# A second set of modulation vectors on TensorE, and the dense layer's first weights loaded one stage earlier

## The chip, the cores and the metric

The kernel runs on one core of a Trainium2 chip. The metric is the device time of one execution in microseconds (us). Five engines work side by side, each through its own instructions in order: TensorE (PE in the profile, with PEld for the loading of its weights), VectorE (DVE), ScalarE (ACT), GpSimd (POOL) and SyncE (SP), which issues most of the DMA transfers.

## The reference

Two layers of a diffusion backbone work on 512 latent and 256 context tokens of 1024 channels, in float32. Each layer is modulated by six vectors that come from a conditioning vector, one set for the latent tokens and one for the context:

```python
mod = silu(c) @ w_ada[l] + b_ada[l]            # 1024 x 6144, and the same with c_ctx
sh1, sc1, g1, sh2, sc2, g2 = split(mod, 6)
h = rms_norm(x, norm1_g[l]) * (1 + sc1) + sh1
p = split_cols(h @ w_in[l], GROUP_COLS)
y = [hgrn2(p[0]), rwkv7(p[1]), window_attention(p[2]), latent_attention(p[3])]
x = x + g1 * (concat(y) @ w_out[l])
h2 = rms_norm(x, norm2_g[l]) * (1 + sc2) + sh2
x = x + g2 * (swiglu(h2) if l == 0 else moe_swiglu(h2))
```

hgrn2 and rwkv7 are recurrences over the tokens, in both directions. The dense SwiGLU of layer 0 has 2816 hidden units; layer 1 has eight experts, of which each token takes two. The output is the final RMSNorm of the latent tokens.

## The kernel before, in words

The activations lie channels x tokens: eight tiles of 128 channels and 768 tokens. Large products are made of three passes: each operand is split into a high part (a cast on ACT, L259) and a low part (the difference, a subtraction on VectorE or POOL, L260), and `mm3` (L270) adds high x high, low x high and high x low. The passes stand as L272, L273 and L274 in the profile. `load_split` (L262) loads a weight tile of 512 KB (`raww`, by SP's queue) and splits it into `hiw` and `low`.

Layer 0 goes through these stages, in times of the profile: modulation, norm and input projection (to about 288); the recurrences of both directions, the attentions' preparation beside them (about 289 to 579); the attentions and the first two columns of the output projection (580 to 745); the other six columns with gated residuals (745 to 806); the second norm and the dense SwiGLU (806 to 1372). Layer 1 and its experts follow.

The modulation vectors are 48 channel tiles for each layer. They are computed in two ways.

- `ada` (L395) uses TensorE. Its weights are `wada`, groups of four channel tiles. The two conditioning vectors are the weights of a matmul of 32 columns, and four such matmuls use the four column quarters of the array, each for every fourth part of the sum (L406, tiles 128x32). ACT copies the four partial sums (L410, `adams`), TensorE transposes them (L413), and VectorE adds the quarters up (L417) and adds the bias (L418). Groups 0 to 3, the first norm's vectors, come at the start of the layer; groups 4 and 5 (the gate g1) come in `modulation` (L1398), beside the recurrences.
- `ada_rest` (L420) uses VectorE. Its weights are `wadt`, one channel tile of 128x1024 each, and the sum is one scaled sum (L436) for each of the two vectors with the vector spread over all partitions (`cb`). `spread` (L314) makes the two `cb` at the first step: 16 transposes (L319) into four PSUM tiles. It has 72 tiles: 24 for the second half of layer 0 (`mod2`: sh2, sc2, g2), 48 for layer 1. 16 of them come in the output projection, by the numbers of `AD` (L1277), the other 56 in the dense layer.

`weave` (L241) lays the streams of the recurrences stage into one program: RWKV's two directions one step a round each, HGRN and the attentions' preparation a fraction of a step, the modulation 6 steps in 122 rounds. The framework's scheduler then orders the instructions of each engine by the buffers and dependencies, and each engine goes through its list in order. A buffer of a pool comes free when its last reader is done; a pool opened on memory that others held waits for those.

In `mixers` (L1502 to L1521) the output projection loads the weights of a column and the input of its residual (`xo`), multiplies, adds the residual on VectorE (L1271), and collects the squares for the norm (`sumsq`). `ffn` (L1526) opens its own weight pool `fw`, loads the first three weight tiles, makes the norm's factors (`norm_rs`, L467 to L472) and its modulated tiles (`norm`, L490 to L492: `hhi` on ACT, `hlo` on VectorE), and goes through pairs of up products, gated units and down products.

Of the kernel before, what the change touches and what calls it, by code (L numbers as in the profile page):

```python
# [11 lines left out]
F32 = mybir.dt.float32  # L12
# [22 lines left out]
# columns of the per-layer parameter block  # L35
# [4 lines left out]
# columns of the constant block  # L40
# [7 lines left out]
def _consts():  # L48
    """Constants that depend on shapes alone."""
# [9 lines left out]
    def rot(n):  # L59
        # out = lhsT.T @ x with out[first quarter] = -x[second], out[second] = x[first]; period n  # L60
        q = n // 4
        r = np.zeros((128, 128), np.float32)
        for p in range(128):
            if (p // q) % 2 == 0:
                r[p + q, p] = -1.0
            else:
                r[p - q, p] = 1.0
        return r
# [35 lines left out]
def _col_tiles():  # L104
    """Column tiles (lists of w_in columns) that are computed channels x tokens, and the token-major group."""
# [17 lines left out]
# heads 0, 2, 1, 3  # L123
# [3 lines left out]
_ADA = [8 * s + 2 * a + i for a in range(4) for s in range(2) for i in range(2)] + list(range(16, 24))  # L127


def _pack(inp):  # L130
# [7 lines left out]
    # shifts and scales of two channel tiles side by side  # L138
    wt = wa[0].reshape(KT, 128, 48, 128)[:, :, _ADA].reshape(KT, 128, 6, 512)
    o['wada'] = wt.transpose(2, 1, 0, 3)  # L140
    o['wadt'] = wa.transpose(0, 2, 1).reshape(48 * L, 128, D)[24:]
# [81 lines left out]
class Ker:  # L223
# [19 lines left out]
    def weave(*gens):  # L243
        """Traces several streams side by side: (generator, steps at a time)."""
# [31 lines left out]
    def gemm_col(s, ps, parts, act, segs):  # L276
        """ps[:, tokens] = weights^T act for one tile of 128 output channels.  parts: (first k, tiles) of the weights."""
# [22 lines left out]
    def diag(s, out, lhsT, rhs, start=True, stop=True):  # L300
        """64 x 64 products of the two partition halves, each with its own half."""
# [3 lines left out]
    def dtrans(s, out, x, idm):  # L305
        """64 x 64 transposes of the two partition halves."""
# [24 lines left out]
    def seg_gemm(s, lhsT, rhs, ntok, use, tag=None):  # L331
        """use(columns, psum) for each segment of lhsT^T rhs; lists of operands are summed."""
# [46 lines left out]
    def setup_masks(s):  # L379
        """The constants that the recurrences need."""  # L380
# [7 lines left out]
        # masks of the pairs that hold the diagonal as well  # L388
# [6 lines left out]
    def ada(s, gs, room, tag, ms):  # L395
        """Groups gs of four channel tiles of the first layer; the four column quarters of the array take every fourth part of the sum.
        room(): where two parts of the weights go; ms(): where the sums of the quarters go."""
        E, V, S = s.E, s.V, s.S
        for g in gs:
# [14 lines left out]
            for h in range(2):  # L414
                at = _ADA[4 * g + 2 * h]
                m = s.mods[0][:, at:at + 2]
                V.tensor_reduce(m, ps[:, 256 * h:256 * h + 256].rearrange("p (j q v) -> p j v q", j=2, q=4)[:, :, :2], AX.X, OP.add)  # L417
                V.tensor_tensor(m, m, s.prm[:, 0, P_BADA + at:P_BADA + at + 2][:, :, None].to_broadcast([128, 2, 2]), OP.add)  # L418

    def ada_rest(s, tp, room):  # L420
        """The first layer's second half and the second layer, a channel tile at a time, without the tensor engine.
        s.adaw(): where the weights of a tile go."""
# [4 lines left out]
        for n in range(72):  # L427
            l, i = divmod(24 + n, 48)
            m = s.mods[1][:, i] if l else s.mod2[:, i - 24]
            w = s.adaw()  # L430
            s.Q.dma_start(w, s.I['wadt'][n])
            # the second layer's context goes no further than its keys
            vs = (0, 1) if l == 0 or i < 16 else (0,)
# [3 lines left out]
            for a, b, nv in ((24, 40, 2), (40, 48, 2), (48, 64, 2), (64, 96, 1)):  # L437
                if 25 + n == b:
                    m = s.mod2[:, a - 24:b - 24] if a < 48 else s.mods[1][:, a - 48:b - 48, :nv]
                    at = P_BADA + a % 48  # L440
                    V.tensor_tensor(m, m, s.prm[:, a // 48, at:at + b - a][:, :, None].to_broadcast([128, b - a, nv]), OP.add)
            yield

# [1 line left out]
    def sumsq(s, m, n, pool, x=None, eng=None):  # L445
        """Adds the squares of channel tile m of the residual to s.acc."""
# [31 lines left out]
    def norm(s, l, mod, sh, sc, gcol, wp, rs, hhi, hlo, ks, ts=None):  # L478
        """Channel tiles ks of the normalised and modulated residual in two parts; ts: room for two tiles."""
# [18 lines left out]
    def proj(s, l, cols, eng=None):  # L498
        """Column tiles (number, tokens) of the input projection into PSUM (channels x tokens); several at once go k by k."""
# [4 lines left out]
    def proj_tok(s, l, it, vt):  # L504
        """HGRN inputs and window values, tokens on partitions."""
# [1465 lines left out]
```

## Time and profile before

| | |
|---|---|
| time, three runs | 2634.31, 2638.28, 2647.7 us; median 2638.28 |
| span of the profiled execution | 2644.5 us (its time around the span isn't listed; the span is 6.2 us above the median) |
| TensorE busy | 2408.1 us, 91% of the span |
| VectorE busy | 1660.6 us, 63% |
| ACT busy | 1227.3 us, 46% |
| POOL busy | 484.9 us, 18% |
| DMA | 322.46 MB, mean 122 GB/s |

The table is the whole program's; the stages differ. A stretch of the program is read with the busy time of each engine in it and the clock that TensorE was granted (1.00 is 2.4 GHz, 0.50 is 1.2 GHz). A row of a timeline has the start, the length, the engine, the source line, and in brackets how long the engine stood idle before it and which instruction ended that. "x8" means so many instructions of one kind in a row. A float32 matmul shows as two records.

### The profile page before, as it was taken

The numbers are of one execution on the slowest core, as the hardware profiler recorded it, in microseconds if no ns is written. First come the engines' busy times: TensorE is split into PE (matmuls) and PEld (weight loads), VectorE is DVE, ScalarE is ACT, GpSimd is POOL, SyncE is SP. The second block draws the span as 40 slices with busy tenths as digits, with TensorE's granted clock in tenths as the row PEclk, the third lists the DMA queues.
The fourth block names the chain that finished last, engine by engine and source line by source line (L and its number), as shares of the span: only waits on it lengthen the run. The fifth ranks groups of instructions, "written<-read, shape, count | busy, mean of one in ns | idle before, by whom it ended". The sixth has DMA issues, their size and how long they took to land. (4 is left out here: it accounts for less than half of the span.)

```text
span 2644.5 us, 46379 instructions
## 1 busy us (share of the span) xinstructions
PE 2408.1 (91%) x18131; PEld 1998.6 (76%) x18131; DVE 1660.6 (63%) x3055; ACT 1227.3 (46%) x2331; POOL 484.9 (18%) x613
## 2 busy tenths in 40 slices
PE   6999788879998999999999997888996999999994
PEld 3889666656586888888888786666674898899993
DVE  5573598777578644344336746876745667667765
ACT  4373356546723211211234654664653556555653
POOL 1010464441011000000020005654102000000002
PEclk9999899989998999999999998998998899999997
DMA  6223110111053433334322130001113888888885
GB/s 245 65 89 111 49 34 20 30 65 57 1 178 129 144 112 120 117 116 132 118 81 64 57 116 13 20 16 49 56 36 107 267 270 270 280 265 264 260 277 179
DMA packets 161026, 322.46 MB, mean 122 GB/s; under 512 B 12288, under 2 KB 84736, under 8 KB 160800
## 3 DMA queue, kind: packets, MB, share of 16 engines
q1 hardware_dynamic: 153744, 293.60, 34.2%
q0 software_dynamic: 6480, 23.73, 2.5%
q8 instruction: 144, 2.36, 0.4%
q10 hardware_dynamic: 576, 2.10, 0.2%
q14 instruction: 82, 0.67, 0.1%
HBM read 295.39 MB, written 22.54 MB: 120 GB/s over the span
## 5 line engine op out<-in xcount | busy, mean ns | idle before, releaser
L272 PE MATMUL big<-hhi,hiw 128*128 128x512 f32 (+1 forms) x1504 | 520.8, 347 | 9.1 <-ACT hhi L491 4.6
L273 PE MATMUL big<-hlo,hiw 128*128 128x512 f32 (+1 forms) x1504 | 523.6, 348 | 2.4 <-DVE hlo L492 2.4
L274 PE MATMUL big<-hhi,low 128*128 128x512 f32 (+1 forms) x1504 | 519.5, 346 | 5.8 <-DVE low L260 3.9
L259 ACT CAST hiw<-raww 128x512 fp32r<-128x512 f32 (+3 forms) x208 | 158.4, 769 | 616.9 <-PE big L273 413.4
L272 PEld LDWEIGHTS big<-hhi,hiw 128*128 128x128 f32 x1504 | 286.2, 191 | 53.2 <-ACT hhi L491 5.7
L274 PEld LDWEIGHTS big<-hhi,low 128*128 128x128 f32 x1504 | 286.2, 190 | 45.1 <-DVE low L260 5.6
L273 PEld LDWEIGHTS big<-hlo,hiw 128*128 128x128 f32 x1504 | 286.4, 190 | 41.0 <-DVE hlo L492 4.2
L260 DVE TENSOR_TENSOR lom<-rawm,him 128x1024 fp32r<-128x1024 f32 x176 | 215.1, 1225 | 128.0 <-ACT him L259 126.7
L260 DVE TENSOR_TENSOR low<-raww,hiw 128x512 fp32r<-128x512 f32 (+3 forms) x196 | 177.3, 909 | 161.1 <-ACT hiw L259 160.8
L259 ACT CAST him<-rawm 128x1024 fp32r<-128x1024 f32 x176 | 184.3, 1047 | 150.4 <-PE sml L273 60.7
L272 PE MATMUL sml<-xh,him 128*128 128x256 f32 x528 | 152.0, 288 | 0.0
L273 PE MATMUL sml<-xl,him 128*128 128x256 f32 x528 | 149.5, 283 | 0.0
L274 PE MATMUL sml<-xh,lom 128*128 128x256 f32 x528 | 149.4, 283 | 0.0
L260 DVE TENSOR_TENSOR lov<-rawv,hiv 128x1024 fp32r<-128x1024 f32 x88 | 107.5, 1222 | 38.2 <-ACT hiv L259 37.8
L272 PE MATMUL sml<-him,xh 128*128 128x256 f32 x440 | 127.4, 290 | 0.7 <-DVE xl L260 0.6
L273 PE MATMUL sml<-lom,xh 128*128 128x256 f32 x440 | 125.4, 285 | 0.0
L274 PE MATMUL sml<-him,xl 128*128 128x256 f32 x440 | 125.3, 285 | 0.0
L273 PE MATMUL big<-gl,hiw 128*128 128x512 f32 (+1 forms) x352 | 119.5, 339 | 0.0
L272 PE MATMUL big<-gh,hiw 128*128 128x512 f32 (+1 forms) x352 | 118.9, 338 | 0.0
L274 PE MATMUL big<-gh,low 128*128 128x512 f32 (+1 forms) x352 | 118.2, 336 | 0.0
L259 ACT CAST hiv<-rawv 128x1024 fp32r<-128x1024 f32 x88 | 92.4, 1050 | 51.3 <-PE y L274 41.5
L757 POOL TENSOR_TENSOR Gm<-G,mskf 128x256 f32<-128x256 f32 x120 | 99.5, 836 | 85.7 <-PE a L612 82.5
(560 smaller groups left out, 5633.7 us busy)
## 6 DMA issues: line engine op xcount, KB each, us to landing
rawm<-in_m SPq DMA_DIRECT2D x176, 512.0 KB, 5.1
rawv<-in_m SPq DMA_DIRECT2D x88, 512.0 KB, 4.7
raww<-in_wadt SPq DMA_DIRECT2D x56, 512.0 KB, 3.5
raww<-in_w SPq DMA_DIRECT2D x52, 512.0 KB, 3.9
raww<-in_winc SPq DMA_DIRECT2D x92, 256.0 KB, 2.8
raww<-in_wout SPq DMA_DIRECT2D x16, 512.0 KB, 4.1
wadt<-in_wadt SPq DMA_DIRECT2D x16, 512.0 KB, 4.4
raww<-in_w SPq DMA_DIRECT2D x16, 448.0 KB, 3.3
```

Source lines behind the costliest of these rows:

```text
L259: s.S.copy(hi, src)
L260: (eng or s.V).tensor_sub(lo, src, hi)
L272: s.E.matmul(out, ah, bh, start=start, stop=False)
L273: s.E.matmul(out, ah, bl, start=False, stop=False)
L274: s.E.matmul(out, al, bh, start=False, stop=stop)
L757: P.tensor_mul(x, G[:, :, 0, :, 0], s.mskf[:, 1 - d, i][:, None, None].to_broadcast(sh))
```

## The change

Groups 6 to 11, the 24 channel tiles of `mod2`, join `wada`. A new function `ada_beside` computes groups 4 to 11 beside the recurrences, in 16 halves of 256 columns: one DMA of 1 MB for each (rows of 1 KB), eight matmuls, a copy, two transposes, a reduction and an add. It has one buffer for the weights and one for the copied sums, and 32 steps in 118 rounds of `weave`. `ada_rest` keeps the 48 tiles of layer 1, all of them in the dense layer, so its spread comes there too. The pool `fw` is opened ahead of the output projection, and three weight tiles of the dense layer are loaded and split in the program's text behind columns 3, 4 and 5.

```diff
-_ADA = [8 * s + 2 * a + i for a in range(4) for s in range(2) for i in range(2)] + list(range(16, 24))
+_ADA = [8 * s + 2 * a + i for a in range(4) for s in range(2) for i in range(2)] + list(range(16, 48))
...
+    def ada_beside(s, gs, room, tag):
+        E, V, S = s.E, s.V, s.S
+        for g, h in itertools.product(gs, range(2)):
+            w, q = room()
+            s.Q.dma_start(w, s.I['wada'][g, :, :, 256 * h:256 * h + 256])
+            yield
+            ps = tag()
+            for k in range(KT):
+                j = 32 * (k % 4)
+                E.matmul(ps[j:j + 32, :256], s.scp[:, k], w[:, k], start=k < 4, stop=k >= 4, tile_position=(0, j))
+            S.copy(q, ps[:, :256])
+            yield
+            ps = tag()
+            for j in range(2):
+                E.transpose(ps[:, 128 * j:128 * j + 128], q[:, 128 * j:128 * j + 128], s.idn)
+            at = _ADA[4 * g + 2 * h]
+            m = s.mods[0][:, at:at + 2] if at < 24 else s.mod2[:, at - 24:at - 22]
+            V.tensor_reduce(m, ps[:, :256].rearrange("p (j q v) -> p j v q", j=2, q=4)[:, :, :2], AX.X, OP.add)
+            V.tensor_tensor(m, m, s.prm[:, 0, P_BADA + at:P_BADA + at + 2][:, :, None].to_broadcast([128, 2, 2]), OP.add)
...
-        for n in range(72):
-            l, i = divmod(24 + n, 48)
-            m = s.mods[1][:, i] if l else s.mod2[:, i - 24]
+        for i in range(48):
+            m = s.mods[1][:, i]
             w = s.adaw()
...
-    AD = 0, 1, 3, 3, 3, 3, 3, 0
...
-                        yield s.ada(range(4, 6), lambda: tp.tile([128, 2, 512], F32, name="wada", bufs=3),
-                                    lambda: s.ps("hg", 512, 2), lambda: tp.tile([128, 512], F32, name="adams")), 6 / 122
+                        yield s.ada_beside(range(4, 12), lambda: [tp.tile([128, *n], F32, name=f"wada{len(n)}") for n in ((KT, 256), (256,))],
+                                           lambda: s.ps("hg", 512, 2)), 32 / 118
...
+                    s.fw = s.fx.enter_context(s.pool("fw", side="right"))
+                    s.floaded = []
                     s.rest = s.ada_rest(s.fx.enter_context(s.pool("fa", side="right")), lambda: s.big())
...
-                            for _ in range(s.AD[m]):
-                                next(s.rest)
+                            if m in (3, 4, 5):
+                                s.floaded.append(s.ffn_load(*s.FIRST[m - 3]))
...
+    FIRST = (0, 0), (0, 1), (1, 0)
+    def ffn_load(s, f, u, eng=None):
+        return [(0, s.load_split(s.fw, s.I['w13'][f, :, u], [128, KT, 128], "w", 3, 4, eng))]
...
-                first, early = [(0, 0), (0, 1), (1, 0)], [(1, 1), (2, 0)]
-                loaded = [load(*x) for x in first]
+                first, early = s.FIRST, [(1, 1), (2, 0)]
+                loaded = s.floaded
```

TensorE in the recurrences, before: the first products of group 4 (L406) between the small products of RWKV (tiles a and c) and HGRN (hg).

```order
L612 MATMUL hg<-it,ket 64x128 x5
L612 MATMUL a_2713<-AP_2400,TT_2646 64x64 x4
L612 MATMUL hg<-it,ket 64x128 x3
L406 MATMUL hg<-wada,scp 32x512 x4
L312 MATMUL a_2706<-cst,TT_2700 128x128 x2
L612 MATMUL c_2751<-rwvt,G 64x128 x2
L612 MATMUL c_2751<-acc,G 64x128 x2
L808 MATMUL c_2751<-Z_2259,ARf_2044 64x64 x4
L312 MATMUL a_2762<-cst,BK_2634 128x128 x4
L312 MATMUL a_2768<-cst,TU_2474 128x128 x2
L612 MATMUL a_2795<-TP_2398,Gm_2683 64x64
L612 MATMUL a_2786<-TP_2261,Gm_2782 64x64
```

TensorE at about the same place now; the new products are L430, their transposes L435 (in the kernel as changed, lines stand some 20 further down).

```order
L430 MATMUL hg<-wada_2513,scp 32x256 x8
L632 MATMUL a_2591<-TP_2261,Gm_2516 64x64 x4
L312 MATMUL a_2598<-cst,TU_2487 128x128 x2
L632 MATMUL hg<-XQ_2300,dd 64x64 x8
L632 MATMUL a_2628<-TP_2411,Gm_2542 64x64 x3
L632 MATMUL a_2620<-AP_2263,TT_2571 64x64 x4
L632 MATMUL a_2628<-TP_2411,Gm_2542 64x64
L312 MATMUL a_2635<-cst,TU_2289 128x128 x2
L632 MATMUL a_2710<-AR_2657,BK_2665 64x256
```

Four products of 512 columns of one group stood in one place, and the next of it elsewhere; now all eight of a half, of 256 columns, stand together, and this place comes 16 times.

VectorE at the start of the output projection, before: the last division of the attentions (L1092), the residuals of columns 0 and 1 (L1271), the low parts of two columns' weights (L260), then the scaled sums (L436).

```order
L1092 RECIPROCAL sm<-sm 128x1
L1271 SCALAR_TENSOR_TENSOR xm_65<-sc,mod_93,xo 128x512
L1271 SCALAR_TENSOR_TENSOR xm_65<-sc,mod_93,xo 128x256
L1271 SCALAR_TENSOR_TENSOR xm_65<-sc,mod_93,xo 128x512
L1271 SCALAR_TENSOR_TENSOR xm_65<-sc,mod_93,xo 128x256
L260 TENSOR_TENSOR low<-raww,hiw 128x1024 x2
L436 SCALAR_TENSOR_TENSOR wadp,mod_95<-wadt,cb_7705 128x1024
L436 SCALAR_TENSOR_TENSOR wadt,mod_95<-wadt,cb_7706 128x1024
```

VectorE there now: L1112 is that division, L503 the norm's factor nA, L1291 the residual; the first three of L260 are the dense layer's tiles.

```order
L1112 RECIPROCAL sm<-sm 128x1
L503 SCALAR_TENSOR_TENSOR nA<-mod_95,prm 128x16
L260 TENSOR_TENSOR low<-raww,hiw 128x1024 x3
L1291 SCALAR_TENSOR_TENSOR xm_65<-sc,mod_93,xo 128x512
L1291 SCALAR_TENSOR_TENSOR xm_65<-sc,mod_93,xo 128x256
L1291 SCALAR_TENSOR_TENSOR xm_65<-sc,mod_93,xo 128x512
L1291 SCALAR_TENSOR_TENSOR xm_65<-sc,mod_93,xo 128x256
L260 TENSOR_TENSOR low<-raww,hiw 128x1024 x2
L1291 SCALAR_TENSOR_TENSOR xm_66<-big,mod_93,xo 128x512
L1291 SCALAR_TENSOR_TENSOR xm_66<-big,mod_93,xo 128x256
L260 TENSOR_TENSOR low<-raww,hiw 128x1024
```

The scaled sums are gone, and three subtractions for the dense layer stand ahead of the first residuals.

TensorE at the start of column 2, before: the end of columns 0 and 1 (sc), the spread (L319), the first passes of column 2.

```order
L272 MATMUL sc<-hhi,hiw 128x256
L273 MATMUL sc<-hlo,hiw 128x256
L274 MATMUL sc<-hhi,low 128x256
L319 MATMUL big<-cst,scp 128x128 x16
L272 MATMUL big<-hhi,hiw 128x512
L273 MATMUL big<-hlo,hiw 128x512
L274 MATMUL big<-hhi,low 128x512
L272 MATMUL big<-hhi,hiw 128x256
```

TensorE in the dense layer now, at the end of the second pair of up products:

```order
L274 MATMUL big<-hhi,low 128x512
L272 MATMUL big<-hhi,hiw 128x256
L273 MATMUL big<-hlo,hiw 128x256
L274 MATMUL big<-hhi,low 128x256
L319 MATMUL big<-cst,scp 128x128 x16
L272 MATMUL big<-hhi,hiw 128x512
L273 MATMUL big<-hlo,hiw 128x512
L274 MATMUL big<-hhi,low 128x512
L272 MATMUL big<-hhi,hiw 128x256
```

The spread left the head of the output projection and stands between the second and the third pair of up products. On SP's queue, the loads of the modulation tiles left the output projection, and four loads of the dense layer, two of modulation tiles and one more of the dense layer stand between the weights of column 3 and the residual's input of column 2.

## Rows read from the trace of the kernel before

**Rows 1.** Windows: stretch, length, busy of PE, PEld, DVE, ACT, POOL; clock, DMA.

```profile
289.00:579.00 290.00, 234.92 (x3352) 177.96 (x3353) 244.47 (x581) 157.45 (x450) 152.58 (x213) 0.92 0.11 34
330.00:355.00 25.00, 23.86 (x354) 17.09 (x352) 23.03 (x55) 15.58 (x46) 18.81 (x25) 1.00 0.26 86
455.00:480.00 25.00, 24.03 (x323) 17.62 (x319) 17.74 (x50) 14.44 (x38) 9.23 (x18) 0.93 0.15 44
745.00:806.00 61.00, 55.01 (x309) 47.26 (x308) 60.34 (x83) 15.37 (x19) 15.05 (x6) 0.97 0.57 185
845.00:1372.00 527.00, 525.16 (x2990) 459.47 (x2990) 237.28 (x320) 109.94 (x124) 19.66 (x11) 1.00 0.38 121
```

**Rows 2.** Timeline of PE, output projection: start, us, instruction, [idle before, releaser].

```profile
747.61 1.93 PE L319 MATMUL big<-cst,scp 128*128 128x128 f32 x16 [2.02 <-DVE xm L1271]
...
749.30 0.48 PE L272 MATMUL big<-hhi,hiw 128*128 128x512 f32 x1
...
749.85 0.40 PE L274 MATMUL big<-hhi,low 128*128 128x512 f32 x1
...
776.88 0.50 PE L274 MATMUL big<-hhi,low 128*128 128x512 f32 x1 [1.68 <-DVE low L260]
...
796.21 0.50 PE L274 MATMUL big<-hhi,low 128*128 128x512 f32 x1 [2.25 <-DVE low L260]
...
798.45 0.63 PE L272 MATMUL big<-hhi,hiw 128*128 128x512 f32 x1
...
805.68 0.28 PE L274 MATMUL big<-hhi,low 128*128 128x256 f32 x1
```

**Rows 3.** Timeline of PE, norm ahead of the dense layer.

```profile
809.74 1.02 PE L467 MATMUL big<-cst,acc 128*128 128x1 f32 x8 [3.78 <-DVE acc L456]
...
817.26 0.79 PE L272 MATMUL big<-hhi,hiw 128*128 128x512 f32 x1 [2.92 <-ACT hiw L259]
...
817.85 0.63 PE L273 MATMUL big<-hlo,hiw 128*128 128x512 f32 x1
```

**Rows 4.** Groups of VectorE's instructions, 745 to 808: count, busy us, mean ns.

```profile
L436 DVE SCALAR_TENSOR_TENSOR wadp<-wadt,cb 128x1024 f32<-128x1024 f32 x16 | 22.8, 1424 | 0.0
L436 DVE SCALAR_TENSOR_TENSOR wadt<-wadt,cb 128x1024 f32<-128x1024 f32 x16 | 22.8, 1424 | 0.4
```

**Rows 5.** Timeline of VectorE, first residuals and norm.

```profile
745.27 2.19 DVE L1271 SCALAR_TENSOR_TENSOR xm<-sc,mod,xo 128x512 f32<-128x512 f32 x4 [18.89 <-PE sc L274]
...
747.38 2.35 DVE L260 TENSOR_TENSOR low<-raww,hiw 128x1024 fp32r<-128x1024 f32 x2
...
814.37 1.80 DVE L490 SCALAR_TENSOR_TENSOR nt<-xm,nA,big 128x512 f32<-128x512 f32 x3 [0.78 <-PE big L472]
...
816.09 1.14 DVE L492 SCALAR_TENSOR_TENSOR hlo<-nt,mod,hhi 128x512 fp32r<-128x512 f32 x2
```

**Rows 6.** Timeline of ScalarE, norm.

```profile
815.15 1.12 ACT L491 ACTIVATE hhi<-nt,mod 128x512 fp32r<-128x512 f32 x2 [1.76 <-DVE nt L490]
```

**Rows 7.** Timeline of SP's queue, first modulation tiles of the output projection.

```profile
730.60 1.28 SPq L431 DMA_DIRECT2D wadt<-in_wadt  x3
```

**Rows 8.** Timeline of VectorE, gated product of the dense layer's first pair.

```profile
845.79 0.95 DVE L1552 TENSOR_TENSOR fs<-fs,big 128x768 f32<-128x768 f32 x1 [1.03 <-ACT fs L1551]
```

**Rows 9.** Timeline of PE in the recurrences.

```profile
467.49 1.06 PE L406 MATMUL hg<-wada,scp 128*32 128x512 f32 x8
...
468.48 0.44 PE L612 MATMUL c<-rwvt,G 128*64 128x128 f32 x4
...
476.02 0.44 PE L413 MATMUL hg<-cst,adams 128*128 128x128 f32 x2
...
476.38 0.44 PE L612 MATMUL hg<-it,att 128*64 128x128 f32 x4
```

**Rows 10.** One line's instructions, L417: ns min/median/max, first and last start.

```profile
L417 DVE TENSOR_REDUCE mod<-hg x4: 156/166/174, 381.2 to 519.4; 128x4 f32<-128x16 f32 x4
```

**Rows 11.** DMA issues: count, size, median us to landing.

```profile
wada<-in_wada SPq DMA_DIRECT2D x8, 512.0 KB, 4.8
```

More of the change, by code (lines that the diff above doesn't have):

```diff
@@ L137, in _pack @@
     wa = f['w_ada']
-    wt = wa[0].reshape(KT, 128, 48, 128)[:, :, _ADA].reshape(KT, 128, 6, 512)
+    wt = wa[0].reshape(KT, 128, 48, 128)[:, :, _ADA].reshape(KT, 128, 12, 512)
     o['wada'] = wt.transpose(2, 1, 0, 3)
-    o['wadt'] = wa.transpose(0, 2, 1).reshape(48 * L, 128, D)[24:]
+    o['wadt'] = wa.transpose(0, 2, 1).reshape(48 * L, 128, D)[48:]
     tiles, tm = _col_tiles()
@@ L415, in ada @@
                 at = _ADA[4 * g + 2 * h]
-                m = s.mods[0][:, at:at + 2]
+                m = s.mods[0][:, at:at + 2] if at < 24 else s.mod2[:, at - 24:at - 22]
                 V.tensor_reduce(m, ps[:, 256 * h:256 * h + 256].rearrange("p (j q v) -> p j v q", j=2, q=4)[:, :, :2], AX.X, OP.add)
                 V.tensor_tensor(m, m, s.prm[:, 0, P_BADA + at:P_BADA + at + 2][:, :, None].to_broadcast([128, 2, 2]), OP.add)
+    def ada_beside(s, gs, room, tag):
[14 more added lines that the diff above has]
+            at = _ADA[4 * g + 2 * h]
+            m = s.mods[0][:, at:at + 2] if at < 24 else s.mod2[:, at - 24:at - 22]
+            V.tensor_reduce(m, ps[:, :256].rearrange("p (j q v) -> p j v q", j=2, q=4)[:, :, :2], AX.X, OP.add)
+            V.tensor_tensor(m, m, s.prm[:, 0, P_BADA + at:P_BADA + at + 2][:, :, None].to_broadcast([128, 2, 2]), OP.add)
     def ada_rest(s, tp, room):
@@ L426, in ada_rest @@
             s.spread(cb[v], s.scp[:, :, v], room)
-        for n in range(72):
-            l, i = divmod(24 + n, 48)
-            m = s.mods[1][:, i] if l else s.mod2[:, i - 24]
+        for i in range(48):
+            m = s.mods[1][:, i]
             w = s.adaw()
-            s.Q.dma_start(w, s.I['wadt'][n])
-            vs = (0, 1) if l == 0 or i < 16 else (0,)
+            s.Q.dma_start(w, s.I['wadt'][i])
+            vs = (0, 1) if i < 16 else (0,)
             for v in vs:
@@ L436, in ada_rest @@
                 V.scalar_tensor_tensor(x, w, 1.0, cb[v], op0=OP.mult, op1=OP.mult, accum_out=m[:, v:v + 1])
[L437 to L441, printed above, removed]
+            for a, b, nv in ((0, 16, 2), (16, 48, 1)):
+                if i + 1 == b:
+                    m = s.mods[1][:, a:b, :nv]
+                    at = P_BADA + a
+                    V.tensor_tensor(m, m, s.prm[:, 1, at:at + b - a][:, :, None].to_broadcast([128, b - a, nv]), OP.add)
             yield
@@ L1505, in mixers @@
                         s.moe_begin(l, wp)
-                    s.adaw = lambda: wp.tile([128, D], F32, name="wadt", bufs=3)
                     for m in range(KT):
@@ L1530, in ffn @@
             hlo = hh.tile([128, KT, T], F32R, name="hlo")
-            with s.pool("fg") as gp, s.pool("fw") as wp:
+            wp = s.fw
+            with s.pool("fg") as gp:
                 def load(f, u):
-                    return [(0, s.load_split(wp, s.I['w13'][f, :, u], [128, KT, 128], "w", 3, 4, s.P if (f, u) in early else None))]
-                first, early = [(0, 0), (0, 1), (1, 0)], [(1, 1), (2, 0)]
-                loaded = [load(*x) for x in first]
+                    return s.ffn_load(f, u, s.P if (f, u) in early else None)
+                first, early = s.FIRST, [(1, 1), (2, 0)]
+                loaded = s.floaded
                 s.adaw = lambda: wp.tile([128, KT, 128], F32, name="raww", bufs=4).rearrange("p a b -> p (a b)")
```

## The prediction

> **What bounds the kernel now.** I read the busy time by stage first, then the output projection instruction by instruction on TensorE and VectorE, last the places in the recurrences where the modulation products already stand. By stage [rows 1], TensorE is the limit of the dense layer: 525.16 of the 527.00 us from 845 to 1372. What VectorE saves there is worth nothing, and what TensorE gets in addition there costs its full length. The output projection (745 to 806) is also TensorE's, 55.01 of 61.00 us, but VectorE is busy for 60.34 of the 61 and TensorE waits for it: 2.02 us at the start, 1.68 and 2.25 us for a low part of the weights, 3.78 us for the last residual and its squares [rows 2, 3]. VectorE's load there is the 32 scaled sums of the modulation tiles, 1424 ns each: 16 of them, 22.8 us, write the scratch tile, 16 more the weight tile itself [rows 4]. In the recurrences (289 to 579) no engine is full: TensorE 234.92 us, VectorE 244.47 of 290.00 us, two in-order engines that feed each other. That is where the changed kernel puts new TensorE work, so the answer is a difference: what the output projection gives back, less what the recurrences and the dense layer pay.
>
> **The output projection.** The 16 transposes of the spread go from its head. TensorE can then begin column 2 at 747.61 instead of 749.30, but the first product that needs a low part waits for the first of two subtractions that start at 747.38 and take 2.35 us together [rows 5], so until about 748.6; it ran at 749.85 [rows 2]. Gain 1.25 us. With the scaled sums gone, the two waits for low parts go: 1.68 + 2.25. Behind the second of them a matmul of 512 columns is busy for 0.63 us (798.45) where others of that shape take 0.40 (749.85) [rows 2]. That is the lower clock for eight matmuls from 797.6 on: at 1.2 GHz 512 columns take 0.43 us, at 2.4 GHz 0.21, so 8 x 0.21 = 1.7, of which I take 1.6; and I take it that the clock doesn't fall where no wait precedes. Sum 1.25 + 1.68 + 2.25 + 1.6 = 6.8 us: the last matmul, at 805.68, moves to about 798.9. Behind it the residual of column 7 no longer stands behind two scaled sums. The first segment's half of that column is done some 3 us ahead of the last matmul, so the 3.78 us of waiting [rows 3] shrink to something between 0 and 1.1 us (a residual, its square and an add for the last segment); I take 0.6, a gain of 3.2. The norm's chain from there (transposed reciprocals, first normalised tile at 814.37 [rows 5]) keeps its length, since its links are one instruction each on ACT, VectorE and TensorE. At its end the first product of the dense layer waits 2.92 us, at the last for a cast of weights [rows 3]; with three weight tiles cast ahead, the bound is the first tile's own high part (ACT from 815.15 [rows 6]) and low part (VectorE from 816.09, about 0.66 us for the larger half [rows 5]), so the second product starts at about 816.75 where it stood at 817.85 [rows 3]: 1.1 us. Sum of this part: 6.8 + 3.2 + 1.1 = 11.1 us gained.
>
> Its bounds: without the regained clock, and with the last wait at 1.1 us, 8.9; with the whole of the 3.78 us and 2.02 us, 13.5. What is late next is the low part of column 2, above, which stands behind the first residuals either way. The three moved tiles bring three subtractions on VectorE ahead of those residuals, and four loads on SP between the fourth load of the projection's weights and the residual's inputs. They lie in the 18.89 us in which VectorE waits for TensorE before 745.27 [rows 5]. Their memory is that of the attentions; the loads of before that took such memory were issued at 730.60 [rows 7]. With 4 to 5 us to land, three casts and three subtractions of about 1.2 us, the last is done near 741 to 743. If that cover is missed, each microsecond beyond 745.27 delays the residuals and TensorE by one; two would be a bad case. Low end of the gain therefore 7.
>
> **The dense layer.** The spread moves behind the second pair of up products. Its 16 transposes took 749.30 - 747.61 = 1.7 us on TensorE [rows 2], and it needs four PSUM tiles, two of which are free only after the product of the second gated tile, which starts when the last up product has ended and takes 0.95 us [rows 8]: with the activation and the hand-over about 1.5 us of waiting. Together 3.2, and 0.3 for the clock behind a wait: 3.5 us. Bounds: 1.7 if another matmul stream hides the wait, 7 if the half clock follows (1.6) and the weights fall behind: on SP the load of the sixth pair stands behind modulation tiles whose buffers come free by scaled sums, and those now wait for the spread. The 48 scaled sums less (24 tiles of two) save nothing, as VectorE has room there.
>
> **The recurrences.** Before, two groups make six blocks of products and four pairs of transposes. A block takes about 1.0 us whatever it holds (467.49 to 468.48), a pair 0.36 us (476.02 to 476.38) [rows 9]: 6 x 1.03 + 4 x 0.36 = 7.6 us of TensorE. After, 16 half groups of eight products with half the columns, the same columns per array part as one block: 16 x 1.0 + 16 x 0.36 = 21.8, and four of the blocks are cut by other work, about 0.55 each: 24.0. TensorE gets 16.4 us more. VectorE gets 12 more pairs of a reduction (166 ns [rows 10]) and an add of like size, 3.9 us; ACT some 4 us of copies, at 157.45 of 290 us.
>
> How much of 16.4 shows in the end? Two stretches hold three blocks each [rows 1]. From 330 to 355, VectorE was busy 23.03 of 25 us, above the stage's 21.1 per 25: the blocks cost nothing. From 455 to 480, TensorE was full (24.03) and VectorE fell to 17.74: 3.3 us of its work late, or at the stage's pace 4.0 us lost for 3.4 us of modulation work. By the first the new work costs 0, by the second 16.4 x 4.0/3.4 = 19.3, with VectorE's 3.9 on top 23. The stage lies between the two stretches in TensorE's load (81%, against 95 and 96), so neither is nearer; I take half of the TensorE price, 9.3, and a quarter of VectorE's, 1.0: 10.3. A small loss of time could also turn into a gain: the granted clock was 0.92 in the stage and 1.00 in the first stretch [rows 1]. The missing 0.08 of 234.92 us is 19 us; a quarter of it regained by a busier TensorE would bring 5, so the low end is -5.
>
> The recurrences' tiles are 128x64 and the new ones 128x32, so the new blocks switch twice each. The row shows 0.99 us for a block [rows 9], whose passes alone are 0.85 at the faster of the two clocks: about 0.07 per switch, and it is in the sum. The Trainium skill, TensorEngine Tiling (Array Packing), section Tiling Modes, Key Properties, says that a change of the tiling mode, not merely of the tile, drains TensorE. If that drain were a whole pass of 512 columns, 0.21 us, instead of the 0.07 of the row, 30 switches more than before would add 30 x 0.14 = 4 us and the sum would be +7, an estimate inside the range; the row speaks for the smaller price.
>
> **Sum.** -11.1 + 3.5 + 10.3 = +2.7 us against the profiled execution, whose span is 2644.5, 6.2 us above the median of 2638.28 and inside the runs' spread of 2634.31 to 2647.7. The terms are differences within one execution, so I put them on the median: 2641 us. Nothing behind the dense layer changes its work.
>
> **Rivals.**
> - The recurrences hide everything, as in 330 to 355: -11.1 + 3.5 = -7.6, so 2630.7. For it: 55 us without TensorE work in the stage, and POOL and ACT half idle. Against it: 455 to 480.
> - The recurrences pay every block as in 455 to 480: +23 + 3.5 - 11.1 = +15.4, so 2654, slower than before. The place is TensorE's queue: the recurrences' small products stand behind each block, VectorE behind those. It decides from a price of about 1.3 us per half group up. For it: VectorE's 84% leaves little to catch up with.
> - One weight buffer: a load of 1 MB goes out only when the previous half's products have read it, and lands after about 5 us (4.8 for the 512 KB loads of before [rows 11]). The half groups stand some 18 us apart on average, so it fits; where two stand 8 us apart, or SP holds the load behind one that waits for the attentions' buffers, TensorE waits in order with everything behind it, up to 5 us. Three such places make +15 on top of half the price of the blocks: about 2652.
> - More than I see is regained (the clock of the recurrences): 2638.3 - 7.6 - 5 = 2626.
>
> **Chances.** My forecast, 2634 to 2648: 0.55. All hidden: 0.18. All paid: 0.15. The weight buffer: 0.07. More regained: 0.05. About 0.5%, 13 us, is what a measurement of this kernel can tell from no change. Faster by that (below 2625) takes the last case or the second with the high end of the projection's gain: 0.13. Slower (above 2651) takes the second and third rivals: 0.19. Within: 0.68. Range for 8 in 10: 2627 to 2654; the forecast's own is 2634 to 2648.
>
> **What would show it.** Output projection: no idle time for low parts, last matmul some 7 us earlier relative to the first residual, L467's counterpart within 1.1 us of it. Start of the dense layer: no wait for a cast. After the second pair: a spread with 1 to 2 us of idle time ahead. Recurrences: 16 blocks of about 1 us, and the stage's length from the first new block to the attentions 5 to 15 us longer. I am wrong if the stage is not longer or by over 19 us, if TensorE waits there for a load of the modulation weights, or if the residuals of the first two columns wait for the moved subtractions.

## The result, and the profile after

The changed kernel takes 2626.76 us (median of 6 runs, 2624.51 to 2628.29); the kernel before, with three more runs beside it, 2638.76. The ratio is 0.9946, 95% interval [0.9933, 0.9959]: 12 us faster, where 2641 was forecast; 2626.76 is just below the low end of the range, 2627. Of the rivals it lies between the one in which the recurrences hide everything (2630.7) and the one in which more is regained than seen (2626).

By stage, in the profile of the changed kernel (windows with the columns of [rows 1]: the recurrences, the output projection from the first residual to the norm's first tile, the dense layer):

```profile
289.80:573.00 283.20, 235.63 (x3604) 176.75 (x3606) 237.91 (x604) 163.69 (x465) 151.43 (x212) 0.97 0.26 79
738.10:799.70 61.60, 55.98 (x309) 48.48 (x307) 17.22 (x26) 14.77 (x19) 11.91 (x6) 0.94 0.24 73
800.00:1362.20 562.20, 558.84 (x3184) 489.45 (x3184) 240.24 (x331) 125.80 (x149) 21.47 (x12) 0.99 0.35 109
```

The recurrences now end 283.2 us after their start, where they took 289.6 before, with some 250 more TensorE instructions, the same busy time of TensorE (235.63, against 234.92 in [rows 1]) and a granted clock of 0.97 in place of 0.92. (These are one execution of each; what further ones show stands with e5 and e11.) VectorE's 60.34 of 61 us in the output projection have become 17.22 of 61.6.

TensorE from the output projection to the second pair of up products (timeline; L487 and L492 are the norm's products, L467 and L472 before):

```profile
740.45 0.47 PE L272 MATMUL big<-hhi,hiw 128*128 128x512 f32 x1 [2.02 <-DVE xm L1291]
...
742.72 0.63 PE L272 MATMUL big<-hhi,hiw 128*128 128x512 f32 x1
...
792.33 0.28 PE L274 MATMUL big<-hhi,low 128*128 128x256 f32 x1
795.07 1.04 PE L487 MATMUL big<-cst,acc 128*128 128x1 f32 x8 [2.45 <-DVE acc L476]
...
801.27 1.65 PE L272 MATMUL big<-hhi,hiw 128*128 128x512 f32 x3 [1.60 <-ACT hhi L511]
802.72 0.63 PE L273 MATMUL big<-hlo,hiw 128*128 128x512 f32 x1
...
830.32 0.50 PE L274 MATMUL big<-hhi,low 128*128 128x512 f32 x1 [0.90 <-POOL low L260]
...
838.36 1.91 PE L319 MATMUL big<-cst,scp 128*128 128x128 f32 x16
840.02 0.48 PE L272 MATMUL big<-hhi,hiw 128*128 128x512 f32 x1
```

Both waits for low parts are gone. From the first residual to the norm's first product it is now 795.07 - 738.10 = 57.0 us, before 809.74 - 745.27 = 64.5 [rows 3, 5]: 7.5 us. Column 2 begins without the spread, but at 742.72 matmuls of 512 columns already take 0.63 us: the lower clock, which stood behind the last wait before [rows 2], now stands behind the wait at the head, in this execution. The spread costs 840.02 - 838.36 = 1.66 us in the dense layer, with no idle time ahead of it.

VectorE there:

```profile
728.46 2.46 DVE L260 TENSOR_TENSOR low<-raww,hiw 128x1024 fp32r<-128x1024 f32 x2 [4.74 <-ACT hiw L259]
731.38 1.23 DVE L260 TENSOR_TENSOR low<-raww,hiw 128x1024 fp32r<-128x1024 f32 x1 [0.46 <-ACT hiw L259]
738.10 2.20 DVE L1291 SCALAR_TENSOR_TENSOR xm<-sc,mod,xo 128x512 f32<-128x512 f32 x4 [5.49 <-PE sc L274]
...
792.65 1.14 DVE L1291 SCALAR_TENSOR_TENSOR xm<-big,mod,xo 128x512 f32<-128x512 f32 x2 [7.18 <-PE big L274]
```

The moved subtractions are done 5.5 us ahead of the first residuals. The last row is the one I had not foreseen: both halves of the last residual run in one piece, released by the last matmul (792.33 above).

In the recurrences, a half group's products and transposes, and the landing of its weights (first the timeline of TensorE, then the line of the loads):

```profile
353.63 1.07 PE L430 MATMUL hg<-wada,scp 128*32 128x256 f32 x16
354.63 0.44 PE L312 MATMUL a<-cst,TU 128*128 128x128 f32 x2
...
360.83 0.38 PE L435 MATMUL hg<-cst,wada 128*128 128x128 f32 x2
361.14 0.45 PE L632 MATMUL a<-TP,Gm 128*64 128x64 f32 x8
```

```profile
L425 SPq DMA_DIRECT2D wada<-in_wada x16: 539/540/669, 288.7 to 534.8; - x16
DMA to landing us min/median/max: 5.8/6.1/7.2
```

A block takes 1.00 us (353.63 to 354.63) and a pair of transposes 0.31 (360.83 to 361.14), about as worked out, so the work put in is the forecast's 16 us; no matmul waits for a load.

### The profile page after: what moved, and what is told of

Read it like the earlier page. It is cut to its first block, busy times and chain, and to the rows that moved or that the text cites. A ratio compares the mean times of both kernels' runs of the same rounds, so it can differ in the third digit from the quotient of the medians.

```text
span 2624.5 us, 46769 instructions
## 1 busy us (share of the span) xinstructions
PE 2402.5 (92%) x18379; PEld 1991.8 (76%) x18379; DVE 1587.8 (61%) x2981; ACT 1233.4 (47%) x2347; POOL 479.6 (18%) x613
## 5 line engine op out<-in xcount | busy, mean ns | idle before, releaser
L273 PEld LDWEIGHTS big<-hlo,hiw 128*128 128x128 f32 x1504 | 285.7, 190 | 41.1 <-DVE hlo L512 4.2
L260 DVE TENSOR_TENSOR lom<-rawm,him 128x1024 fp32r<-128x1024 f32 x176 | 215.3, 1225 | 125.8 <-ACT him L259 121.8
L260 DVE TENSOR_TENSOR low<-raww,hiw 128x512 fp32r<-128x512 f32 (+3 forms) x196 | 172.5, 884 | 179.5 <-ACT hiw L259 179.3
L260 DVE TENSOR_TENSOR lov<-rawv,hiv 128x1024 fp32r<-128x1024 f32 x88 | 107.6, 1223 | 40.5 <-ACT hiv L259 40.5
```

The lines of the kernel that those rows point to most:

```text
L260: (eng or s.V).tensor_sub(lo, src, hi)
L273: s.E.matmul(out, ah, bl, start=False, stop=False)
```

## The experiments

Three theories stood against each other for the recurrences. The forecast: half of the new work is paid. A: the denser stream keeps TensorE's clock at 2.4 GHz, and that pays for the work. B: the work fills idle time, and the clock was chance. "Time at 1.2 GHz" is summed from the trace's record of the granted clock, without the stretch that runs over the end of the stage in every profile; "stage" is the length of the recurrences of layer 0. The diffs are cut to the lines that matter, with "..." for what is left out.

**The recurrences' part alone** (e1), on the kernel before:

```diff
-                        yield s.ada(range(4, 6), ...), 6 / 122
+                        yield s.ada_beside(range(4, 12), ...), 32 / 118     # 12 results go to mod2b
```

> The kernel before, with the 16 half groups of products beside the recurrences (in place of the two groups), their 12 additional results going to a tile that nobody reads; all else, VectorE's own 24 tiles in the output projection too, as before. It is the change in the recurrences alone. Forecast of the prediction (half of the work is paid): +10 us. Theory A (the denser stream of TensorE work keeps the granted clock at its upper level; the time at 1.2 GHz in the recurrences falls from 41 us to about 14, which pays for the 16 us of new work): -3 us, clock in the stage 0.95 or more. Theory B (the work fills idle time of TensorE, and the clock of the one profile was chance): 0 within 2 us.

Measured: 2641.54 us against 2640.77, ratio 1.0000 [0.9987, 1.0012]. The stage, by its window:

```profile
287.70:572.20 284.50, 237.13 (x3603) 177.86 (x3605) 238.39 (x604) 163.71 (x465) 151.55 (x211) 0.97 0.26 78
```

It costs nothing within 3 us, so the forecast's +10 falls. The clock is up as A says (17.1 us at 1.2 GHz). The time is B's 0; A's -3 lies at the edge of the interval.

**Fillers in place of the products** (e2), on the kernel before: TensorE's part without anything else.

```diff
+    def filler(s, n, tag):
+        for _ in range(n):
+            ps = tag()
+            for k in range(KT):
+                j = 32 * (k % 4)
+                s.E.matmul(ps[j:j + 32, :256], s.scp[:, k], s.cst[:, :256], start=k < 4, stop=k >= 4, tile_position=(0, j))
+            yield
+            yield
...
+                        yield s.filler(16, lambda: s.ps("hg", 512, 2)), 32 / 118
```

> The kernel before, with 16 blocks of eight products 32x256 beside the recurrences that use constants already on the chip and whose results nobody reads: TensorE's part of the new work without its transfers, copies, transposes and VectorE instructions, some 16 us of TensorE in addition to all of before. Forecast of the prediction: +8 us. Theory A (clock): -4 us, since nothing but the clock changes for the better, with under 20 us at 1.2 GHz in the stage where before had 41. Theory B (idle time): 0 within 2 us.

Measured: ratio 1.0002 [0.9990, 1.0014]. 23.9 us at 1.2 GHz, where A named under 20; stage 289.2. Again B's time, and A's direction of the clock.

**Every half's products twice** (e3), on the changed kernel:

```diff
-            for k in range(KT):
+            for k in [*range(KT), *range(KT)]:
```

> The changed kernel with the eight products of every half group done twice in a row (the second time over the first): 16 us more of TensorE in the recurrences, no further load, copy or VectorE work. It asks where the room ends. Forecast's price (half): +8 us against the changed kernel. Theory A: the clock is regained already (14 us at 1.2 GHz left), so little more comes back and the blocks, twice as long, are paid for a good part: +5 to +12. Theory B: TensorE still has some 40 us without work, 0 to +3.

Measured: 2639.57 us, ratio to before 0.9993 [0.9981, 1.0006]: 10 to 13 us slower than the changed kernel's 2626.76 to 2629.45, for 16 us of work.

```profile
290.20:589.80 299.60, 257.34 (x3859) 190.79 (x3861) 240.39 (x604) 162.55 (x463) 150.90 (x211) 0.94 0.25 75
```

TensorE is busy for 257.34 us of 299.60. The time is at the upper end of A's +5 to +12, and B's 0 to +3 falls: the room that the change uses is used up. The clock of 0.94 (30.7 us at 1.2 GHz) says nothing against A by itself, since two profiles with the single halves have as much (e7, e11).

**The recurrences of before, the rest as changed** (e4):

```diff
-                        yield s.ada_beside(range(4, 12), ...), 32 / 118
+                        yield s.ada(range(4, 6), ...), 6 / 122
...
+        V.memset(s.mod2, 0.0)
```

> The changed kernel with the recurrences of before: two groups of products, as before; the 24 vectors of the second half of layer 0 are left out (set to zero), everything from the output projection on as changed. Against the kernel before it shows the change without the recurrences: the trace of the changed kernel gives -9.4 us for that part (-7.5 to the norm, -1.9 in the dense layer). Theory A: 2629 (-9.5), 3 us slower than the changed kernel. Theory B: 2627, as the changed kernel. Forecast of the prediction: -7.6 against before, and 10 us faster than the changed kernel (2617).

Measured: 2626.94 us, ratio 0.9947 [0.9930, 0.9963]. The whole gain is here: the change's price in the recurrences is nil within the interval, its gain all behind them. The forecast's 2617 falls; between A's 2629 and B's 2627 this run can't tell, as both lie in the interval. That the vectors are zero here and in e8 does not show in what follows: from the first to the last product of the experts it is 546.1 and 546.4 us, in the changed kernel 545.6.

**The kernel before once more** (e5), unchanged.

> The kernel before once more, for a second profile and more runs. If the stretches at 1.2 GHz in the recurrences (41 us in the first profile) belong to this order of instructions, some 35 to 45 us stand there again and the stage takes 286 to 290 us; if they were chance, anything from 14 up. From the first residual of the output projection to the norm's first tile: 69 to 70 us, as before. Time 2640 within 3.

Measured: ratio 1.0003 [0.9992, 1.0014].

```profile
289.40:573.80 284.40, 229.93 (x3357) 174.09 (x3359) 242.92 (x580) 156.87 (x449) 151.24 (x212) 0.95 0.11 34
```

The same order has 27.3 us at 1.2 GHz this time and a stage of 284.4, 5.2 shorter than in the first profile, below the 35 to 45 expected. So most of the 6.4 us between the first two profiles' recurrences (289.6 and 283.2) was chance.

**Without the earlier weight pool** (e6), on the changed kernel:

```diff
-                    s.fw = s.fx.enter_context(s.pool("fw", side="right"))
...
-                            if m in (3, 4, 5):
-                                s.floaded.append(s.ffn_load(*s.FIRST[m - 3]))
...
-                loaded = s.floaded
+                loaded = [load(*x) for x in first]
```

> The changed kernel without the part that opens the weight pool ahead of the output projection: the pool is opened in the dense layer and the three tiles are loaded there in the program's text, as before. The scheduled order of every engine comes out the same as the changed kernel's, row for row (the loads move up by themselves, since the memory of the modulation tiles is no longer taken); only addresses differ. So, by every theory, the time of the changed kernel, 2627 within 3, and this part of the change has no effect of its own. If an address or a pool's bound mattered after all: up to 5 us slower. It also gives a second profile of the changed order: 14 to 20 us at 1.2 GHz in the recurrences and 283 to 285 us for the stage by theory A, anything by theory B.

Measured: 2629.54 us, ratio 0.9954 [0.9940, 0.9967], as the changed kernel. The pool's move has no effect of its own that could be seen: once the modulation tiles' three buffers are gone, the loads move up by themselves. In this profile the lower clock at the projection's head is missing, though the order is the changed kernel's, and first residual to norm is 55.5 us: the clock's fall there is worth 1.5 us.

**The spread back at the projection's head** (e7), on the changed kernel:

```diff
             s.spread(cb[v], s.scp[:, :, v], room)
+        yield
...
+                            if m == 1:
+                                next(s.rest)
```

> The changed kernel with the 16 transposes of the spread at the head of the output projection, where they were before, and not in the dense layer. A theory on the gain of the output projection: all of it is the sums' removal, and the spread costs the same 1.7 us at either place, so 0 against the changed kernel within the measurement's 3 us; the first modulation tiles' sums then stand in the output projection again (eight, 10 us of VectorE), and should do no harm, since VectorE has 40 us without work there. A rival: the head of the output projection is the dearer place (4 us: the transposes, the wait, and what the clock loses): +3 to +5.

Measured: 2630.57 us, ratio 0.9965 [0.9952, 0.9977], 1 to 4 us above the changed kernel. The head of the projection (timeline of TensorE):

```profile
745.03 1.93 PE L319 MATMUL big<-cst,scp 128*128 128x128 f32 x16 [2.02 <-DVE xm L1292]
746.72 0.48 PE L272 MATMUL big<-hhi,hiw 128*128 128x512 f32 x1
...
748.33 0.40 PE L274 MATMUL big<-hhi,low 128*128 128x512 f32 x1
```

The transposes take their 1.7 us, but no matmul of 0.63 us follows, and from first residual to norm it is 57.1 us, as in the changed kernel: there the lower clock takes what the spread's removal gave. The time lies between the expected 0 and the rival's +3 to +5 and decides for neither.

**The removal alone** (e8), on the kernel before:

```diff
-        for n in range(72):
+        yield
+        for n in range(24, 72):
...
-    AD = 0, 1, 3, 3, 3, 3, 3, 0
+    AD = 0, 1, 0, 0, 0, 0, 0, 0
```

> The kernel before with the 24 modulation tiles of the second half of layer 0 left out (the vectors are set to zero): no loads and no scaled sums for them in the output projection and the dense layer; the spread stays at the head of the output projection, the recurrences are as before. It is the removal alone. Theory: the removal is the whole gain, 2627 to 2629, as with the recurrences of before and the rest changed (2627). Rival: a part of the gain is the moved spread, 2631 or more.

Measured: 2631.22 us, ratio 0.9962 [0.9949, 0.9976]; first residual to norm 57.1 us. The removal of the 48 scaled sums and their loads is 10 of the 12 us; whether the rest is the spread's new place is within what these runs can't tell (e6, in the same series: 2629.54).

**Fillers at the start of both recurrences** (e9), on the changed kernel (the filler of e2, with one yield a block):

```diff
                 def modulation(tp):
+                    yield s.filler(6, lambda: s.ps("hg", 512, 2)), 1
                     if l == 0:
```

> The changed kernel with six blocks of eight products on constants, results unread, at the very start of the recurrences of both layers, where TensorE has little to do and where most stretches at 1.2 GHz that are left stand (10 us in layer 0, 17 in layer 1 of the changed kernel's profile). Within one order of instructions the stage's length so far went with the time at 1.2 GHz in it, about 0.37 us per us (before: 27.3 us and 284.4, 41.0 and 289.6; changed: 13.7 and 283.2, 30.7 and 289.3). If that is cause, the 27 us vanish from both starts and give back up to 10 us, less what the blocks cost in the queue (12 blocks of 1 us in stretches where TensorE idles half of the time, 6 us): -4 us against the changed kernel. If the clock is only a sign of waits that have another cause: the blocks' price alone, +3 to +8.

Measured: 2629.05 us, ratio 0.9952 [0.9939, 0.9966]; the changed kernel beside it (e11) 2629.45. The starts of the recurrences of layers 0 and 1, with the fillers and, below, in the changed kernel:

```profile
288.00:320.00 32.00, 26.09 (x352) 15.82 (x354) 29.75 (x56) 15.00 (x41) 24.01 (x35) 1.00 0.27 80
1580.00:1620.00 40.00, 32.44 (x430) 22.86 (x429) 28.64 (x66) 19.52 (x53) 30.08 (x45) 1.00 0.03 12
```

```profile
288.00:320.00 32.00, 19.91 (x220) 12.79 (x219) 27.72 (x51) 13.90 (x36) 23.84 (x35) 0.84 0.26 79
1580.00:1620.00 40.00, 29.66 (x334) 22.43 (x332) 30.60 (x70) 19.47 (x53) 28.82 (x45) 0.79 0.03 11
```

With TensorE kept busy the clock stays up: 1.00 in place of 0.84 and 0.79. It buys nothing: neither the 4 us of gain nor the 3 us of loss came. That the blocks' price and what the clock returns are about even would fit; the two were not separated.

**No modulation products beside the recurrences** (e10), on the changed kernel:

```diff
-                    if l == 0:
-                        yield s.ada_beside(range(4, 12), ...), 32 / 118
+                    return
+                    yield
...
+        V.memset(s.mod2, 0.0)
+        V.memset(s.mods[0][:, 16:24], 0.0)
```

> The changed kernel with no modulation products beside the recurrences at all; the gate and the second set of vectors of layer 0 are left out (zero). With the two groups of before (7.6 us of TensorE) the time was 2626.9, with 16 half groups (24 us) 2626.8 and 2629.5, with twice their products (40 us) 2639.6. Theory A (a price of about a quarter at an equal clock, given back by the clock): none is no faster than two groups, 2626 to 2630, with 35 us or more at 1.2 GHz in the recurrences and a stage of 284 to 288 us. Theory of idle time alone: the stage falls on a flat floor, 2627 too, but with a clock no lower than with two groups. Forecast of the prediction (half of the work is paid): 4 us faster than with two groups, 2623.

Measured: 2697.38 us, but that isn't comparable: without the gate the numbers of layer 1 are others, and from the first to the last product of the experts it is 617.3 us in place of 545.6. (That the tokens go to other experts is the likely cause, and not shown.) Its recurrences can be compared:

```profile
288.00:569.40 281.40, 223.80 (x3316) 174.26 (x3318) 240.78 (x571) 157.29 (x447) 151.31 (x212) 0.93 0.07 20
```

5 us shorter than the mean with two groups and 3 us shorter than the shortest of them. It is one profile: if it stands, these first 7.6 us of products are paid in good part, as the forecast had it, and theory A's "no faster than two groups" doesn't hold. The two stretches in which six of these blocks stood show no such price (rows of e10 below, in the part on why).

**The changed kernel once more** (e11), unchanged.

> The changed kernel once more, beside the two others, for a third profile of its order and more runs: 2627 to 2630. Stage of the recurrences against time at 1.2 GHz on the line of the profiles so far (283.2 at 13.7, 284.4 at 17.1, 289.3 at 30.7), within 1 us.

Measured: 2629.45 us, ratio 0.9957 [0.9943, 0.9970]; 30.7 us at 1.2 GHz and a stage of 287.3, 2 below the line I had drawn.

```profile
289.80:577.10 287.30, 241.66 (x3605) 180.92 (x3607) 238.51 (x603) 164.16 (x465) 151.84 (x212) 0.94 0.25 78
```

Against e5, with about the same time at 1.2 GHz (27.3 us), TensorE is busy 11.7 us longer here and the stage takes 2.9 us more.

All profiles of the recurrences together:

| TensorE work beside the recurrences | stage, us (us at 1.2 GHz) | mean |
|---|---|---|
| none | 281.4 (34.1) | 281.4 |
| two groups, 7.6 us (before, e5, e4, e8) | 289.6 (41.0), 284.4 (27.3), 287.0 (37.5), 285.0 (30.7) | 286.5 (34.1) |
| two groups and 16 filler blocks, 24 us (e2) | 289.2 (23.9) | 289.2 |
| 16 halves, 24 us (after, e1, e6, e7, e11) | 283.2 (13.7), 284.5 (17.1), 284.4 (17.1), 289.3 (30.7), 287.3 (30.7) | 285.7 (21.9) |
| 16 halves and 6 filler blocks, 30 us (e9) | 286.2 (10.2) | 286.2 |
| 16 halves doubled, 40 us | 299.6 (30.7) | 299.6 |

Within a row the stage is longer where more of it ran at 1.2 GHz, by 0.3 to 0.4 us for each. At 30.7 us the halves take 288.3 on average and the one profile with two groups 285.0: some 3 us of price for 16 us of work. On average the halves have 12 us less at 1.2 GHz, worth about 4 if the clock is the cause of the length. The sum is nil. That it is the cause isn't shown: the two profiles with fillers (e2, e9) lie some 3 and 4 us above what the halves' row would give at their time at 1.2 GHz, which can be the fillers' price or a limit of the rule.

## Why the prediction was wrong

**The recurrences, +10.3: the step that failed.** "I take half of the TensorE price, 9.3, and a quarter of VectorE's, 1.0." Measured: ratio 1.0000 [0.9987, 1.0012] for this part alone (0 within 3 us), and -0.8 us by the stage's means. The amount of work was right (1.00 us a block). The price was not, and neither of its two premises holds. The stretch from 455 to 480 was read as VectorE held up by three blocks, 17.74 us of 25. Without any block VectorE is as low there: in e10, whose recurrences start at 288.0, the two stretches read (windows with the columns of [rows 1]):

```profile
330.00:355.00 25.00, 19.50 (x314) 15.20 (x312) 22.53 (x51) 15.05 (x44) 17.08 (x25) 1.00 0.01 2
455.00:480.00 25.00, 20.83 (x299) 16.90 (x300) 18.19 (x50) 16.38 (x41) 12.58 (x19) 0.93 0.08 22
```

VectorE's 18.19 without blocks stand against 17.74 with them, TensorE's 20.83 against 24.03; from 330 to 355 it is 22.53 against 23.03, and 19.50 against 23.86. In both stretches the blocks filled time in which TensorE had stood idle, and VectorE did about the same work beside them; that it does little from 455 to 480 belongs to that part of the stage. So there were not a free and a dear stretch to take the middle of. And the stage's 81% of TensorE does not lie between 95 and 96%, as the text has it: it is below both, which spoke for more room.

The clock was in the text only as the range's low end, -5. It is up by the means (34.1 us at 1.2 GHz with two groups, 21.9 with the halves), and in e9. VectorE's own instructions also got shorter: its busy time in the stage is 242.9 to 243.7 us in the four profiles with two groups and 237.9 to 238.7 in the five with the halves, though these give it 12 more reductions and adds; with the fillers alone (e2), which give it nothing to do, it is 239.1. How much of the even sum is the filled idle time, the clock or this was not separated. None of them alone says why the next 16 us (e3) cost 10 to 13.

**The output projection, -10.0 to the norm: -7.5 measured.** Two terms were mis-sized. The wait ahead of the norm's first product shrank from 3.78 to 2.45 us, a gain of 1.3 and not 3.2: "the first segment's half of that column is done some 3 us ahead of the last matmul" is true, but its residual is released only with the tile's last matmul (the VectorE row at 792.65). And the clock's 1.6 us were not regained: "I take it that the clock doesn't fall where no wait precedes" does not decide it, since the head has a wait of its own, 2.02 us, and the clock fell there instead. It does so in six of the seven profiles without the spread in that place (not in e6), and in one of the six with it (e2; not in before, e1, e5, e7, e8): with the spread the clock falls there less often, and without it not always. The two waits for low parts (1.68, 2.25) went as said. The two shortfalls are 3.5 us together and the difference is 2.5: 1 us more than forecast came elsewhere, some of it at the head, where four products now stand ahead of the first that needs a low part, before two. (The part's bounds, 8.9 and 13.5, come to 9.0 and 13.7 when added up; nothing rests on that.)

**The start of the dense layer, -1.1: right in size, not in the way.** The second pass's first product stands 3.01 us behind the norm's first tile (799.71 to 802.72), before 3.48 (814.37 to 817.85): 0.5 us, where 1.1 was forecast at this very place. But TensorE begins at 801.27 with three first passes in a row, where it did one before, and the fourth up column begins 29.1 us behind the tile, before 30.2: the 1.1 us is there, by an order that the forecast did not have.

**The spread, +3.5: 1.66 measured.** The four PSUM tiles were free: no idle time ahead of the row at 838.36. The feared queue behind the modulation tiles did not show either: behind 836 us no wait of TensorE long enough to be listed is left in the layer.

**Not foreseen.** The fourth tile's low part comes earlier on POOL: TensorE's wait there is 0.90 us now. Before, these rows stood there (timeline of TensorE), a wait of 1.84 and the lower clock behind it:

```profile
847.03 0.50 PE L274 MATMUL big<-hhi,low 128*128 128x512 f32 x1 [1.84 <-POOL low L260]
...
848.97 0.63 PE L272 MATMUL big<-hhi,hiw 128*128 128x512 f32 x1
```

That lower clock stands there in two of the four profiles with the sums (before, e5) and in none of the nine without. By the means of these 4 and 9, the dense layer takes 562.8 and 561.5 us from the norm's first tile to the last residual: -1.3, where -1.1 + 3.5 = +2.4 was forecast. The input stage of layer 1 is 1.0 us shorter in the nine, for which I have no cause. The sum: -7.5 - 1.3 - 1.0 - 0.8 = -10.6, against 11 to 12 us in the runs.

**The rivals.** The weight buffer falls (no wait for a load; six us to land, the shortest interval fits). Its price was also mis-added: 2638.3 - 7.6, half the price of the blocks (9.3 or 10.3) and 15 come to 2655 or 2656, not 2652. "All paid" falls by e1. "All hidden" had the mechanism, and lies 4 us above the result, for terms of its sum that came out otherwise, as said above. That the change doesn't do what it says holds for one part of it: the earlier pool (e6). On the tile mode: by the prediction's estimate of 0.85 us of passes, the block's 1.00 us leaves 0.15 for two changes of mode, as in the sum. The Trainium skill, TensorEngine Tiling (Array Packing), Tiling Modes, Key Properties, says that such a change drains TensorE; the 0.15 us are in keeping with it, and no run here took the changes out to show it.

## What to carry to other kernels

Work moved from a stage that one engine fills (VectorE, 60 of 61 us) into a latency-bound stage where two engines are each some 80% busy can be free up to a point: try the amount, and twice the amount, since a single profile's stretches don't tell where the point lies. Before a slow stretch is put down to the work that stands in it, look at the same stretch without that work: here it was slow without it too (e10). Before a price is read from one execution of such a stage, a second profile of the same kernel is due: here the same order differed by 5 us. And a part of a change that moves program text needs a look at the scheduled order: loads rise by themselves when memory is free.

## What the runs showed of the hardware

- The granted clock in the recurrences differs between executions of one kernel: 41.0 and 27.3 us at 1.2 GHz in two of before, 13.7, 17.1 and 30.7 in three of the changed order.
- VectorE's products on SBUF are not of constant length. The same 16 instructions, before and after (groups of instructions: count, busy us, mean ns):

```profile
L714 DVE TENSOR_TENSOR AR<-W,rwkk 64x252 f32<-64x252 f32 x16 | 10.7, 669 | 0.3
```

```profile
L734 DVE TENSOR_TENSOR AR<-W,rwkk 64x252 f32<-64x252 f32 x16 | 7.9, 496 | 0.2
```

In the trace of before, nine of the sixteen lie for 70% of their length or more beside a POOL instruction; they take 0.81 us on average, from 0.40 to 1.59. The four that lie beside one for less than a tenth take 0.41 to 0.42 each. The Trainium skill, GPSIMD Engine Reference, section Specifications, says that GpSimd's way to SBUF is shared with VectorE where VectorE reads two inputs from SBUF, as these products do; it agrees that only those beside a POOL instruction, wholly or in part, are long; yet some of these are as short as the free ones. No run changed this alone, so what it is worth to the stage is not tested.
